# A hybrid decoder layer with 32 experts: expert weights stored as 16 KB runs and loaded in page pairs, 26 pages in place of 24

## The chip, the cores and the metric

The program runs on one core of a Trainium2 chip, as one launch, with all inputs in HBM. The metric is the device time of one launch in microseconds, the median of several; lower is better.

## The reference

One decoder layer over 256 tokens of 1024 numbers, all float32: projections of x, sparse attention (8 heads) and a gated linear recurrence (4 heads), an output projection, a layer norm, then a mixture of 32 experts of which each token uses 4, and a second layer norm. The change concerns the experts:

```python
logits = xf @ w_r + b_r
top_v, top_i = lax.top_k(logits, TOP_K)          # 4 of 32
top_w = jax.nn.softmax(top_v, axis=-1)
# for the rows xb of expert e:
h = xb @ w_gu[e] + b_gu[e]                       # w_gu[e]: 1024 x 2048
gate = jnp.minimum(h[:, :D_FF], SWIGLU_LIMIT)
up = jnp.clip(h[:, D_FF:], -SWIGLU_LIMIT, SWIGLU_LIMIT)
act = gate * jax.nn.sigmoid(SWIGLU_ALPHA * gate) * (up + 1.0)
y = act @ w_dn[e] + b_dn[e]                      # w_dn[e]: 1024 x 1024
```

An expert has 8.39 MB of w_gu and 4.19 MB of w_dn, 12.58 MB together; 32 experts are 402.7 MB.

## The kernel before

**Two stages.** First the attention and recurrence stage up to the router, about 205 us, whose order is found by a planner while the program is built: `Merge.run` (L205) picks among streams of work, on the planner's own clock, whichever can run next; a stream that asks for buffer space that is not there (`need`, L352) waits. Then the expert loop (L1740) in plain order: for each expert `gate_up` (L1577), `combine` of the expert before, for every second expert a `gather` of the rows of the next two, `scatter_lhs`, then `down` (L1611). The last expert (e31) is written apart (L1793 on), with its weights in smaller pieces.

**Pages.** Buffers come from 24 pages of 8 KB per partition (1 MB), each a tile of its own (class `Pages`, L224). A page can be cut into halves of 1024 and quarters of 512 words. One expert takes twelve pages: `g{e}_0` to `g{e}_7` for w_gu (a page holds 128 rows of 2048 numbers) and `d{e}_0` to `d{e}_3` for w_dn (256 rows of 1024, two to a partition). Twenty pages' worth goes round in the expert loop; two of the halves are used together as one page.

**Loads.** All weights come through one queue, SyncE's (SP). `want` (L367) puts loads in a list; `pump` (L370) issues from its head as long as a page is free, and is called whenever a buffer is freed (`Buf.free`, L344). `wg` and `wd` (L1750, L1758) free the page of the piece before when they ask for the next piece. An issue waits on the chip for the readers of its page, and also for the load that was issued eight loads earlier, since there are eight semaphores for SP's loads. In the first stage `GATE` holds loads back to times of the planner's clock.

**Layout.** `w_gu[e]` and `w_dn[e]` lie in HBM as the reference has them. A load of `g{e}_k` reads one run of 8 KB per partition, a load of `d{e}_k` two runs of 4 KB. For e31 the w_gu pieces have runs of 2 KB, the w_dn pieces runs of 2 KB and 1 KB, and most of these are issued as two or three loads (`fine`, L364).

Of the kernel before, what the change touches and what calls it, by code (L numbers as in the profile page):

```python
# [20 lines left out]
P = 128  # L21
# [8 lines left out]
RMS_EPS = 1e-6  # L30
GELU = float(2.0 * np.sqrt(2.0 / np.pi))
SET_LN_EXP = 'natural_log_exp_and_others'
NPAGES = 24
NR = 4
WARM = 30
GATE = {'wq0': 2.75, 'wq1': 5.75, 'wkg0': 8.75, 'wkg1': 11.5, 'wgh0': 14.5, 'wgh1': 17.5, 'wqa0': 20.25, 'wqa1': 23.25, 'wvs0': 26.25, 'wkv0': 29.0, 'wc00': 32.0, 'wc10': 35.0, 'wc01': 37.75, 'wc11': 40.75, 'wi0': 43.75, 'wi1': 46.5, 'wo2': 49.5, 'wo3': 61.75, 'wo0': 64.5, 'wo1': 69.75, 'bias': 86.0, 'xres': 87.5, 'ln1': 90.25, 'g0_0': 91.0, 'g0_1': 94.0, 'g0_2': 101.75, 'g0_3': 104.5, 'g0_4': 107.5, 'g0_5': 110.5, 'g0_6': 113.25, 'g0_7': 118.0, 'd0_0': 122.0, 'd0_1': 124.75, 'd0_2': 127.75, 'd0_3': 130.75, 'g1_0': 137.5, 'g1_1': 140.25, 'g1_2': 143.25, 'g1_3': 151.0, 'g1_4': 153.75, 'g1_5': 156.75, 'g1_6': 159.75, 'g1_7': 167.25}
# [10 lines left out]
WC_AT = 6  # L47
PARTS = ((4,), (5,), (6, 7))
ROUTER_AT = 'rec'
LAST = [(slice(k * 512, (k + 1) * 512), slice(0, 512), (4, 512)) for k in range(2)]  # L50
LAST += [(slice(None), slice(c, c + 256), (8, 256)) for c in (512, 768)]
# [176 lines left out]
class Pages:  # L228

    def __init__(self, pool, n, clock):
        self.pool, self.clock = pool, clock
        self.tiles, self.kind = [None] * n, [None] * n
        self.whole = list(range(n))
        self.part = {1024: [], 512: []}
        for pg in range(n):
            self.renew(pg, "G")

    def renew(self, pg, kind):  # L240
        if self.kind[pg] != kind:
            self.kind[pg] = kind
            self.tiles[pg] = self.pool.tile([P, 2048], F32, name=f"page{pg}", tag=f"page{pg}")
            self.clock.same[self.tiles[pg].tensor.name] = f"page{pg}"

    def halves(self):
        return 2 * len(self.whole) + len(self.part[1024])

    def fits(self, n, whole=False):
        return bool(self.whole or not whole and (len(self.part[1024]) >= max(1, n // 1024) or n == 512 and self.part[512]))  # L250

    def get(self, n, kind="G", last=False):
        if n == 2048:
            if not self.whole:
                return None
            pg = self.whole.pop(-1 if last else 0)
            self.renew(pg, kind)
            return (pg, 0, 2048)
        if not self.part[n]:
            up = self.get(2 * n, last=True)  # L260
            if up is None:
                return None
            pg, o, _ = up
            self.part[n] += [(pg, o), (pg, o + n)]
        pg, o = self.part[n].pop(0)
        return (pg, o, n)

    def put(self, key):
        pg, o, n = key
        if n == 2048:  # L270
            self.whole.append(pg)
            return
        mate = (pg, o ^ n)
        if mate in self.part[n]:
            self.part[n].remove(mate)
            self.put((pg, min(o, o ^ n), 2 * n))
        else:
            self.part[n].append((pg, o))

    def ap(self, key):  # L280
        pg, o, n = key
        return self.tiles[pg][:, o:o + n]


def shaped(ap, shape):
# [9 lines left out]
def layer(ctx: ExitStack, tc: tile.TileContext, a: dict, out: bass.AP, dbg=None, n_exp=NEXP, cap_limit=CAP):  # L295
# [64 lines left out]
        return Buf(words, key=key)  # L360


    queue, loaded = [], {}
    fine = {f"d{n_exp - 1}_0": ((0, 2), (2, 4)), f"d{n_exp - 1}_1": ((0, 2), (2, 4)), f"d{n_exp - 1}_3": ((0, 4), (4, 6), (6, 8)), "wf1": ((0, 2), (2, 4))}  # L364
    fine.update({f"g{n_exp - 1}_{k}": ((0, 1), (1, 2)) for k in range(KD)})

    def want(name, src, shape, kind="pre"):  # L367
        queue.append((name, src, shape, kind))

    def pump():  # L370
        while queue:
            name, src, shape, kind = queue[0]
            if name == "pk":
                queue.pop(0)
                sp.dma_start(cst, a["cst"])
                sp.dma_start(pk, a["pk"])
                sp.dma_start(ipk, a["ipk"])
                continue
            whole = kind == "pre" or kind == "small" and shape[2] == 2048
            if waiting or mg.now < GATE.get(name, 0.0) or not pages.fits(shape[2] if kind == "small" else 2048, whole):  # L380
                return
            if "att1" not in mg.fired and kind != "small" and pages.halves() - 2 < (RES if GATE else (4, 10)[kind == "exp"]):
                return
            queue.pop(0)
            if kind == "small":
                rows, cols, words_ = shape
                bf = Buf(words_)
                loaded[name] = ([bf], bf.ap[:rows, words_ - cols:])
                sp.dma_start(loaded[name][1], src)
                continue  # L390
            if kind == "pre":
                bf = Buf(2048)
                loaded[name] = ([bf], bf.v(*shape))
                sp.dma_start(loaded[name][1], src)
                continue
            n = shape[0] // 2
            bufs = [Buf(1024), Buf(1024)] if not pages.whole or HALVES and len(pages.part[1024]) > 1 else [Buf(2048)]
            rows, rest = src.shape[0], tuple(shape[1:])
            for u, v in fine.get(name, ((0, shape[0]),) if len(bufs) == 1 else ((0, n), (n, 2 * n))):
# [65 lines left out]


    cst = small("cst", [C_END])
    pkb, ipkb = buf(1024), buf(512)
    pk = pkb.ap[:, :B_END]
    ipk = ipkb.v(dt=I32)[:, :227]  # L470
    lvl, pos_i = shaped(ipk[:, :224].bitcast(U8), (7, 128)), ipk[:, 224:227]
# [46 lines left out]
    for e in range(n_exp):  # L518
        if e == max(n_exp - 2, 0):
            want("ln2", a["ln2"], (4, 512, 2048), "small")  # L520
        for k in range(KD):
            src, shape = a["w_gu"][e, k * 128:(k + 1) * 128, :].rearrange("p (j f) -> p j f", j=2), (2, FF)
            if e == n_exp - 1:
                src = a["w_gu"][e, k % 4 * 256:(k % 4 + 1) * 256, :].rearrange("(a p) (j f) -> p a j f", p=P, j=2)
                src, shape = src[:, :, :, k // 4 * 512:(k // 4 + 1) * 512], (2, 2, 512)
            want(f"g{e}_{k}", src, shape, "exp")
        for k in range(4):
            rows, cols, shape = (slice(k * 256, (k + 1) * 256), slice(None), (2, 1024)) if e < n_exp - 1 else LAST[k]
            want(f"d{e}_{k}", a["w_dn"][e, rows, cols].rearrange("(a p) d -> p a d", p=P), shape, "exp")

    queue.pop(0)
    wf0 = buf(2048)
# [264 lines left out]

    def queries_h():
        yield "q"
        qf = (yield from need(1024))  # L800
        hg["qf"] = qf
        for j in range(2):
            act.copy(qf.v(4, S)[:, 2 * j:2 * j + 2, :], res_bank["q"][j].rearrange("p (h t) -> p h t", h=2))
        drop(*res_bank["q"])
        mg.fire("qf")
# [646 lines left out]
    def gather_first(t):  # L1452
# [29 lines left out]
            dve.tensor_reduce(Wt[:, u, :], ohw.rearrange("p j e -> p e j"), AX.X, OP.add)  # L1482
        swzb = Buf(0, key=scratch["late"][0].key)
        swz.extend([swzb.v(4, 2, 128)[:, j] for j in range(2)])


    def start():
# [55 lines left out]
    alid = small("alid", [128])  # L1543
    pool.tensor_scalar(alid, ident, ALPHA, None, OP.mult)
    sbuf = [small(f"sw{j}", [2, CAP]) for j in range(2)]
    xgb = h1b["xg"].v(KD, 128)
    n_g, n_s = [1], [0]

# [140 lines left out]
    def fallback():  # L1689
# [5 lines left out]
        with tc.If(most > cap_limit):  # L1695
            with tc.For_i(0, n_exp, 1) as ei:
# [6 lines left out]
                def wg(k):  # L1703
                    w_ = wb[n[0] % 3].v()
                    n[0] += 1
                    sp.dma_start(w_, a["w_gu"][eds, k * 128:(k + 1) * 128, :].rearrange("a p f -> p (a f)"))
                    return [w_[:, :FF], w_[:, FF:]]

                def wd(fc):
                    if fc % 2 == 0:  # L1710
                        n[0] += 1
                    w_ = wb[n[0] % 3].v(2, 1024)
                    if fc % 2 == 0:
                        sp.dma_start(w_, a["w_dn"][eds, fc * 128:(fc + 2) * 128, :].rearrange("e (a p) d -> p (e a) d", p=P))
                    return w_[:, fc % 2, :]

                for rd in range(1, S // CAP):
# [130 lines left out]
def arrange(i):  # L1848
# [28 lines left out]
    a["w_gu"], a["w_dn"] = n["w_gate_up"][0], n["w_down"][0]  # L1877
# [17 lines left out]
```

## Time and profile before

| | us |
|---|---|
| median of 3 runs | 1165.85 |
| lowest, highest | 1162.73, 1166.91 |
| the profiled execution | 1166.2 |
| its span, first to last instruction | 1164.4 |
| TensorE (PE) busy | 1059.9 (91%) |
| VectorE, ScalarE, GpSimd busy | 294.7, 200.3, 75.8 |

The profile's page divides the span into 40 slices of 29.1 us: busy tenths of each engine, TensorE's granted clock, the mean busy share of the 16 DMA engines and the GB/s they moved. PE's busy time counts modelled ends of pipelined matmuls; what it waits for is better read from its timeline. The profiled execution stands 0.35 us above the median of the runs.

### The profile page before, as it was taken

To read this page: it belongs to the slowest core of one execution; us is meant where nothing else is said; L and a number is where in the kernel's file an instruction comes from. 1 tells how busy PE (TensorE), PEld (TensorE's weight loads), DVE (VectorE), ACT (ScalarE), POOL (GpSimd) and SP (SyncE) were. 2 spreads that over 40 slices of the span, in tenths; PEclk is the share of its full clock that TensorE was granted. 3 is DMA by queue.
4 is the path that set the end of the run, shared out by engine and by line. 5 is a ranking of instruction groups with operands and counts; after the bars stand their busy time and mean duration, and the time that the engine had idled before them with its cause. 6 is when DMAs were issued, how large, how long until landed. Compare 5 with 4: busy or idle time off the path is not lost. (4 is left out here: it accounts for less than half of the span.)

```text
span 1164.4 us, 13820 instructions
## 1 busy us (share of the span) xinstructions
PE 1059.9 (91%) x5714; PEld 494.0 (42%) x5714; DVE 294.7 (25%) x626; ACT 200.3 (17%) x418; POOL 75.8 (7%) x69
## 2 busy tenths in 40 slices
PE   8788889899999999999999999989898989898986
PEld 8677667334343343434343434333333333332343
DVE  5898886401111111111111111111111111111013
ACT  5565754101010100101010101000000010010101
POOL 5554120000000000000000000000000000000001
PEclk9999999899999999999999999999999999999998
DMA  9721737989999999999999999999999999999993
GB/s 360 320 77 69 290 122 300 386 323 379 415 416 416 416 418 416 417 416 418 416 416 416 417 417 414 418 415 417 417 415 417 415 416 417 416 417 417 413 384 111
DMA packets 85922, 430.04 MB, mean 369 GB/s; under 512 B 7512, under 2 KB 9816, under 8 KB 54496
## 3 DMA queue, kind: packets, MB, share of 16 engines
q1 hardware_dynamic: 85856, 429.13, 91.3%
q8 instruction: 46, 0.75, 0.3%
q14 instruction: 20, 0.16, 0.0%
HBM read 428.05 MB, written 1.05 MB: 369 GB/s over the span
## 5 line engine op out<-in xcount | busy, mean ns | idle before, releaser
L441 PE MATMUL bank<-page,page 128*64 128x512 f32 (+2 forms) x3412 | 753.6, 592 | 29.4 <-DMA page<-in_w_gu 16.7
L441 PEld LDWEIGHTS bank<-page,page 128*64 128x64 f32 (+1 forms) x3412 | 247.4, 142 | 499.1 <-issue 404.5
L1593 DVE TENSOR_SCALAR page<-bank 128x512 f32<-128x512 f32 (+1 forms) x33 | 22.3, 676 | 716.7 <-PE bank L441 716.7
L143 PE MATMUL bank<-page,page 128*128 128x256 f32 (+7 forms) x904 | 143.1, 340 | 10.5 <-DVE page L143 5.0
L143 PEld LDWEIGHTS bank<-page,page 128*128 128x128 f32 (+2 forms) x904 | 116.6, 185 | 27.7 <-DVE page L143 6.4
L1594 ACT ACTIVATE page<-page 128x512 f32<-128x512 f32 (+1 forms) x33 | 20.3, 616 | 462.1 <-DVE page L1593 462.1
L441 PE MATMUL bank<-G,page 128*128 128x128 f32 x480 | 57.6, 278 | 15.1 <-DVE G L1556 15.1
L441 PEld LDWEIGHTS bank<-G,page 128*128 128x128 f32 x480 | 54.7, 192 | 27.5 <-DVE G L1556 27.5
L1810 POOL TENSOR_TENSOR page<-page,page 128x320 f32<-128x320 f32 (+1 forms) x2 | 1.6, 790 | 991.4 <-DVE page L1817 991.4
L143 DVE TENSOR_TENSOR page<-page,page 128x512 fp32r<-128x512 f32 (+5 forms) x62 | 54.7, 922 | 24.7 <-ACT page L143 24.6
L143 POOL TENSOR_TENSOR page<-page,page 128x512 fp32r<-128x512 f32 (+4 forms) x35 | 53.1, 1531 | 90.7 <-ACT page L143 73.2
L1621 ACT COPY page<-bank 128x512 f32<-128x512 f32 x31 | 18.1, 585 | 231.5 <-PE bank L441 231.5
L143 ACT CAST page<-page 128x512 fp32r<-128x512 f32 (+3 forms) x71 | 43.7, 654 | 16.8 <-PE bank L143 10.0
L441 PE MATMUL bank<-cst,sw 128*64 128x128 f32 x256 | 22.0, 295 | 19.1 <-DVE sw L1571 19.1
L1607 ACT COPY page<-bank 128x512 f32<-128x512 f32 (+1 forms) x33 | 18.9, 572 | 77.9 <-PE bank L448 77.9
L1562 ACT COPY page<-bank 128x512 f32<-128x512 f32 x30 | 17.6, 585 | 84.0 <-PE bank L441 84.0
L1574 DVE COPY page<-bank 128x256 f32<-128x256 f32 x32 | 13.6, 425 | 68.4 <-PE bank L441 68.4
L441 PEld LDWEIGHTS bank<-cst,sw 128*64 128x64 f32 x256 | 13.7, 140 | 35.4 <-DVE sw L1571 31.3
L1595 DVE TENSOR_TENSOR page<-page 128x512 f32<-128x512 f32 (+1 forms) x33 | 22.3, 676 | 22.5 <-ACT page L1594 22.5
L143 PE MATMUL bank<-cst,page 128*128 128x128 f32 (+2 forms) x101 | 16.9, 293 | 9.7 <-DVE page L143 8.3
L441 PEld LDWEIGHTS <-i 96*64 96x64 bf16 x197 | 11.0, 109 | 28.2 <-issue 28.0
L1598 DVE SCALAR_TENSOR_TENSOR page<-page 128x512 f32<-128x512 f32 (+1 forms) x33 | 22.3, 676 | 1.1
(148 smaller groups left out, 440.2 us busy)
## 6 DMA issues: line engine op xcount, KB each, us to landing
page<-in_w_gu SPq DMA_DIRECT2D x226, 1024.0 KB, 17.6
page<-in_w_dn SPq DMA_DIRECT2D x112, 1024.0 KB, 17.7
page<-in_w_gu SPq DMA_DIRECT2D x60, 512.0 KB, 16.1
page<-in_w_dn SPq DMA_DIRECT2D x31, 512.0 KB, 15.2
page<-in_w_o SPq DMA_DIRECT2D x4, 1024.0 KB, 4.7
page<-in_w_q SPq DMA_DIRECT2D x2, 1024.0 KB, 9.8
page<-in_w_gh SPq DMA_DIRECT2D x2, 1024.0 KB, 13.3
page<-in_w_qa SPq DMA_DIRECT2D x2, 1024.0 KB, 14.3
```

Source lines behind the costliest of these rows:

```text
L143: r = f(*args, **kw)
L441: pe.matmul(o, l, r, start=start, stop=stop, skip_group_check=True)
L1562: act.copy(xg[:, 4 * q:4 * q + 4, :m * CAP], bk[q].rearrange("p (a b) -> p a b", a=4)[:, :, :m * CAP])
L1574: dve.tensor_copy(sz.rearrange("p a b -> p (a b)"), bk[0][:, :256])
L1593: dve.tensor_scalar(ga, hb[0][:, :n], 7.0, None, OP.min)
L1594: act.activation(sg_, ga, AF.Sigmoid, scale=1.702)
L1595: dve.tensor_tensor(sg_, sg_, ga, OP.mult)
L1598: dve.scalar_tensor_tensor(up, up, 1.0, sg_, OP.add, OP.mult)
L1607: act.copy(aT, bk[0][:, :n * 128].rearrange("p (c s) -> p c s", c=n))
L1621: act.copy(y, py)
L1810: pool.tensor_tensor(z, z, lnp[:, 0, c0:], OP.mult)
```

## The change

The four edits are these. The expert weights are laid out anew on the host: for e0 to e30, two neighbouring pieces (`g{e}_0` and `g{e}_1`, and so on) stand side by side, so that a partition's part of the two is one run of 16 KB; e31 has arrays of its own (`w_gl`, `w_dl`) in which each piece is a run of 8 KB per partition. The pages are tiles of 16 KB per partition, two pages to a tile, and there are 26 in place of 24, from descriptor space of dynamic DMAs that this program does not use (`SCRATCH`). In the expert loop `pump` loads two pieces with one DMA of 2 MB as soon as both pages of a tile are free; pieces of e0 and e1 may go alone. Last, some buffers of the first stage move: `qf` and the router's sums share a page that is set aside from the start, and `alid` and the two `sw` tiles lie in the second half of that page instead of in tiles of their own.

```diff
-NPAGES = 24
+NPAGES = 26
+LAX = 1
+SCRATCH = 1024
...
+    def renew(self, pair, kind):
+        if self.kind[pair] != kind:
+            self.kind[pair] = kind
+            self.tiles[pair] = self.pool.tile([P, 4096], F32, name=f"page{pair}", tag=f"page{pair}")
...
+    def usable(self, kind="G"):
+
+        return [pg for pg in self.whole if self.kind[pg // 2] == kind or pg ^ 1 in self.whole]
+
+    def pairs(self):
+        return [pg for pg in self.whole if pg ^ 1 in self.whole and self.whole.index(pg ^ 1) < self.whole.index(pg)]
...
+    def get(self, n, kind="G", last=False, near=None, apart=False):
+
+        if n == 4096:
+            two = self.pairs()
+            if not two:
+                return None
+            pg = two[0] & ~1
+            self.whole.remove(pg)
+            self.whole.remove(pg + 1)
+            self.renew(pg // 2, kind)
+            return (pg, 0, n)
...
-            bufs = [Buf(1024), Buf(1024)] if not pages.whole or HALVES and len(pages.part[1024]) > 1 else [Buf(2048)]
+            bufs = None
+            if kind == "exp" and name[0] in "gd" and mates.get(name):
+                other = mates[name][0]
+                if int(name[-1]) % 2 == 0 and mg.now >= 1e6:
+                    key = pages.get(4096)
+                    if key is None and int(name[1:-2]) > LAX:
+                        queue.insert(0, (name, src, shape, kind))
+                        return
+                    if key is not None:
+                        queue.pop(0)
+                        two = [Buf(0, key=(key[0] + i, 0, 2048)) for i in range(2)]
+                        sp.dma_start(pages.ap(key), mates[name][1])
+                        for nm, b_ in zip((name, other), two):
+                            loaded[nm] = ([b_], [shaped(b_.ap[:, o:], (n,) + tuple(shape[1:])) for o in (0, 1024)])
+                        continue
+                near = loaded[other][0][0].key[0] ^ 1 if other in loaded else None
+                key = pages.get(2048, near=near, apart=near is None)
+                bufs = key and [Buf(0, key=key)]
+            if not bufs:
+                bufs = [Buf(2048)] if pages.usable() else [Buf(1024), Buf(1024)]
...
-    pkb, ipkb = buf(1024), buf(512)
+    pkb = buf(1024)
+    qf_late = pages.get(2048, near=pkb.key[0] ^ 1)
+    ipkb = buf(512)
...
+                src, shape = a["w_gl"][k].rearrange("p (a j f) -> p a j f", a=2, j=2), (2, 2, 512)
+            else:
+                src, shape = a["w_gu"][e, k // 2, :, k % 2 * 2048:k % 2 * 2048 + 2048].rearrange("p (j f) -> p j f", j=2), (2, FF)
+                mates[f"g{e}_{k}"] = (f"g{e}_{k ^ 1}", a["w_gu"][e, k // 2])
...
-        qf = (yield from need(1024))
+        qf = Buf(0, key=(qf_late[0], 0, 1024))
...
-        scratch["late"][0] = yield from need(1024)
+        scratch["late"][0] = Buf(0, key=(qf_late[0], 1024, 1024))
...
+    a["w_gu"] = gu.reshape(NEXP, 4, 2, P, 2 * FF).transpose(0, 1, 3, 2, 4).reshape(NEXP, 4, P, 4 * FF)
+    a["w_dn"] = dn.reshape(NEXP, 2, 4, P, D).transpose(0, 1, 3, 2, 4).reshape(NEXP, 2, P, 4 * D)
...
+    nc = bacc.Bacc("TRN2", target_bir_lowering=False, num_devices=1, dynamic_dma_scratch_size=SCRATCH)
```

**Place 1, SP's queue in the middle of the loop.** One expert's loads before; `page15_1795` is page 15, `128x2048` the elements written.

```order
L404 DMA page9_75<-in_w_gu 128x2048
L404 DMA page15_1795<-in_w_gu 128x2048
L404 DMA page2_1821<-in_w_gu 128x2048
L404 DMA page20_1857<-in_w_gu 128x2048
L404 DMA page14_1859<-in_w_gu 128x2048
L404 DMA page18_84<-in_w_gu 128x2048
L404 DMA page6_72<-in_w_gu 128x2048
L404 DMA page19_85<-in_w_gu 128x2048
L404 DMA page0_1301<-in_w_gu 128x2048
L404 DMA page3_1331<-in_w_dn 128x2x1024
L404 DMA page4_1363<-in_w_dn 128x2x1024
L404 DMA page5_1395<-in_w_dn 128x2x1024
```

The same place in the changed kernel, where a page name is a pair of pages.

```order
L436 DMA page0_1321<-in_w_gu 128x4096
L436 DMA page2_1386<-in_w_gu 128x4096
L436 DMA page9_75<-in_w_gu 128x4096
L436 DMA page3_69<-in_w_gu 128x4096
L436 DMA page5_71<-in_w_dn 128x4096
L436 DMA page10_76<-in_w_dn 128x4096
```

Twelve loads of 1 MB have become six of 2 MB, and the tiles that go round are eleven pairs, 22 MB, in place of 20 MB.

**Place 2, SP's queue where the first stage ends.** Rows of L143 (before) are issued by the first stage, rows of L404 by the expert loop.

```order
L143 DMA page2_1821<-in_w_gu 128x2048
L143 DMA page20_1857<-in_w_gu 128x2048
L143 DMA page14_1859<-in_w_gu 128x2048
L404 DMA page18_84<-in_w_dn 128x2x1024
L404 DMA page6_72<-in_w_dn 128x2x1024
L404 DMA page19_85<-in_w_dn 128x2x1024
L404 DMA page0_1301<-in_w_dn 128x2x1024
L404 DMA page3_1331<-in_w_gu 128x2048
```

After, with L144 the line of the first stage, and L451 and L436 lines of the loop:

```order
L144 DMA page7_1812<-in_w_gu 128x2048 x2
L144 DMA page11_77<-in_w_dn 128x2048
L144 DMA page4_70<-in_w_dn 128x2048
L451 DMA page6_72<-in_w_dn 128x2048 x2
L436 DMA page8_74<-in_w_gu 128x4096
L436 DMA page0_1321<-in_w_gu 128x4096
```

Two pieces more, `d1_0` and `d1_1`, are asked for before the loop; from the weights of e2 on all loads up to e30 are pairs.

**Place 3, ScalarE (ACT) in the first stage.** The rows with `sm` are a head's softmax exponentials, the CASTs of 128x512 make the split operands of projections, and the eight COPYs of 64x128 move transposed blocks for the recurrence. Before:

```order
L143 ACTIVATE page_74,sm_949<-bank_90,mx_948 128x128 x2
L143 ACTIVATE page_74,sm_949<-bank_97,mx_948 128x128 x2
L143 CAST page_102<-page_76 128x512 x2
L143 COPY page_88<-bank_96 64x128 x8
L143 CAST page_103<-page_78 128x512
L143 ACTIVATE page_74,sm_989<-bank_91,mx_988 128x128 x2
```

After:

```order
L144 ACTIVATE page_69,sm_910<-bank_81,mx_909 128x128 x2
L144 ACTIVATE page_69,sm_910<-bank_82,mx_909 128x128 x2
L144 CAST page_89<-page_69 128x512 x3
L144 COPY page_76<-bank_86 128x2x128
L144 ACTIVATE page_77,sm_964<-bank_80,mx_963 128x128 x2
L144 ACTIVATE page_77,sm_964<-bank_85,mx_963 128x128 x2
L144 CAST page_89<-page_69 128x512
L144 COPY page_75<-bank_79 64x128 x8
```

The eight copies now stand behind the second head's exponentials instead of between the first and the second; the same work stands in another order there, and so on PE and VectorE beside it.

## Rows read from the trace of the kernel before

**Rows 1.** The page: PE's busy time, DMA share and rate by slice.
```profile
PE 1059.9 (91%) x5714; PEld 494.0 (42%) x5714; DVE 294.7 (25%) x626; ACT 200.3 (17%) x418; POOL 75.8 (7%) x69
DMA  9721737989999999999999999999999999999993
GB/s 360 320 77 69 290 122 300 386 323 379 415 416 416 416 418 416 417 416 418 416 416 416 417 417 414 418 415 417 417 415 417 415 416 417 416 417 417 413 384 111
```
**Rows 2.** PE's timeline of the loop: start, length in us, tiles; brackets: idle before.
```profile
319.74 3.84 PE L441 MATMUL bank<-G,page 128*128 128x128 f32 x32 [1.01 <-DVE G L1556]
...
375.73 3.84 PE L441 MATMUL bank<-G,page 128*128 128x128 f32 x32 [1.00 <-DVE G L1556]
...
431.76 3.84 PE L441 MATMUL bank<-G,page 128*128 128x128 f32 x32 [1.00 <-DVE G L1556]
...
605.61 7.09 PE L441 MATMUL bank<-page,page 128*64 128x512 f32 x32 [0.38 <-ACT page L1607]
...
631.73 8.78 PE L441 MATMUL bank<-page,page 128*64 128x512 f32 x32 [0.34 <-ACT page L1607]
...
760.33 1.94 PE L441 MATMUL bank<-page,page 128*64 128x512 f32 x8 [0.43 <-DMA page<-in_w_gu]
...
1075.78 3.84 PE L441 MATMUL bank<-G,page 128*128 128x128 f32 x32 [1.01 <-DVE G L1556]
```
**Rows 3.** PE's waits: what for, us in total, times, longest.
```profile
PE bank L143 <- DVE page L143: 19.3, 10, 3.5
...
PE bank L441 <- DMA page<-in_w_gu: 16.7, 28, 1.4
```
**Rows 4.** Windows: busy us of PE, PEld, DVE, ACT, POOL; clock; DMA share; GB/s.
```profile
0.00:205.00 205.00, 176.15 (x1209) 149.27 (x1209) 157.44 (x328) 115.99 (x275) 72.31 (x65) 0.96 0.57 221
...
265.00:275.00 10.00, 9.66 (x58) 4.21 (x59) 0.42 (x1) 1.88 (x4) 0.00 (x0) 1.00 0.86 307
275.00:300.00 25.00, 23.63 (x112) 8.07 (x110) 3.55 (x7) 1.67 (x3) 0.00 (x0) 0.93 1.01 414
300.00:760.00 460.00, 437.89 (x2258) 171.37 (x2254) 60.01 (x128) 38.74 (x65) 0.00 (x0) 1.00 1.02 416
760.00:1075.00 315.00, 283.96 (x1420) 105.11 (x1420) 39.65 (x84) 24.47 (x41) 0.00 (x0) 0.99 1.02 416
...
1112.00:1130.00 18.00, 15.11 (x92) 7.29 (x93) 0.37 (x1) 1.17 (x2) 0.00 (x0) 0.91 1.05 386
```
**Rows 5.** The page's DMA sections: packets by size, packets by queue, issues by size.
```profile
DMA packets 85922, 430.04 MB, mean 369 GB/s; under 512 B 7512, under 2 KB 9816, under 8 KB 54496
...
q8 instruction: 46, 0.75, 0.3%
...
page<-in_w_gu SPq DMA_DIRECT2D x226, 1024.0 KB, 17.6
```
**Rows 6.** SP's issues of g4, then PE's gate_up of e4, from the timeline.
```profile
282.17 19.13 SPq L404 DMA_DIRECT2D page<-in_w_gu  x10
...
332.78 15.82 PE L441 MATMUL bank<-page,page 128*64 128x512 f32 x72
```
**Rows 7.** Loads by tensor, issue to landing: w_gu first, then w_o.
```profile
DMA to landing us min/median/max: 4.7/17.5/21.4
...
DMA to landing us min/median/max: 4.6/4.7/6.4
```
**Rows 8.** The end: SP's last weight loads; PE's last products of down.
```profile
1123.48 14.64 SPq L404 DMA_DIRECT2D page<-in_w_dn  x8
...
1150.76 2.95 PE L441 MATMUL bank<-page,page 128*64 128x256 f32 x19
```

More of the change, by code (lines that the diff above doesn't have):

```diff
@@ L49 @@
 ROUTER_AT = 'rec'
-LAST = [(slice(k * 512, (k + 1) * 512), slice(0, 512), (4, 512)) for k in range(2)]
-LAST += [(slice(None), slice(c, c + 256), (8, 256)) for c in (512, 768)]
+LAST = [(4, 512), (4, 512), (8, 256), (8, 256)]
 LAST_ORDER = (("p", 0), ("a", 0), ("p", 1), ("p", 2), ("a", 1), ("a", 2))
@@ L233, in __init__ @@
         self.pool, self.clock = pool, clock
-        self.tiles, self.kind = [None] * n, [None] * n
+        self.tiles, self.kind = [None] * (n // 2), [None] * (n // 2)
         self.whole = list(range(n))
         self.part = {1024: [], 512: []}
[L237 to L244, printed above, removed]
+        for pair in range(n // 2):
+            self.renew(pair, "G")
@@ new lines, in renew @@
+    def renew(self, pair, kind):
+        if self.kind[pair] != kind:
+            self.kind[pair] = kind
+            self.tiles[pair] = self.pool.tile([P, 4096], F32, name=f"page{pair}", tag=f"page{pair}")
+            self.clock.same[self.tiles[pair].tensor.name] = f"page{pair}"
+    def usable(self, kind="G"):
+        return [pg for pg in self.whole if self.kind[pg // 2] == kind or pg ^ 1 in self.whole]
+    def pairs(self):
+        return [pg for pg in self.whole if pg ^ 1 in self.whole and self.whole.index(pg ^ 1) < self.whole.index(pg)]
@@ L246, in halves @@
     def halves(self):
-        return 2 * len(self.whole) + len(self.part[1024])
+        return 2 * len(self.usable()) + len(self.part[1024])
     def fits(self, n, whole=False):
-        return bool(self.whole or not whole and (len(self.part[1024]) >= max(1, n // 1024) or n == 512 and self.part[512]))
-    def get(self, n, kind="G", last=False):
+        return bool(self.usable() or not whole and (len(self.part[1024]) >= max(1, n // 1024) or n == 512 and self.part[512]))
+    def get(self, n, kind="G", last=False, near=None, apart=False):
[8 more added lines that the diff above has]
+            return (pg, 0, n)
@@ L253, in get @@
         if n == 2048:
-            if not self.whole:
-                return None
-            pg = self.whole.pop(-1 if last else 0)
-            self.renew(pg, kind)
-            return (pg, 0, 2048)
+            ok = self.usable(kind)
+            if not ok:
+                return None
+            single = [pg for pg in ok if pg ^ 1 not in self.whole]
+            double = [pg for pg in ok if pg ^ 1 in self.whole]
+            first = (double or single) if apart else (single or double)
+            pg = near if near in ok else first[-1 if last else 0]
@@ L259, in get @@
+            self.whole.remove(pg)
+            self.renew(pg // 2, kind)
+            return (pg, 0, n)
         if not self.part[n]:
@@ L269, in put @@
         pg, o, n = key
+        if n == 4096:
+            self.whole += [pg, pg + 1]
+            return
         if n == 2048:
@@ L281, in ap @@
         pg, o, n = key
-        return self.tiles[pg][:, o:o + n]
+        o += pg % 2 * 2048
+        return self.tiles[pg // 2][:, o:o + n]
 def shaped(ap, shape):
@@ L360, in need @@
         return Buf(words, key=key)
-    queue, loaded = [], {}
+    queue, loaded, mates = [], {}, {}
     fine = {f"d{n_exp - 1}_0": ((0, 2), (2, 4)), f"d{n_exp - 1}_1": ((0, 2), (2, 4)), f"d{n_exp - 1}_3": ((0, 4), (4, 6), (6, 8)), "wf1": ((0, 2), (2, 4))}
@@ L396, in pump @@
             n = shape[0] // 2
-            bufs = [Buf(1024), Buf(1024)] if not pages.whole or HALVES and len(pages.part[1024]) > 1 else [Buf(2048)]
+            bufs = None
[5 more added lines that the diff above has]
+                        queue.insert(0, (name, src, shape, kind))
+                        return
+                    if key is not None:
[10 more added lines that the diff above has]
+                bufs = [Buf(2048)] if pages.usable() else [Buf(1024), Buf(1024)]
             rows, rest = src.shape[0], tuple(shape[1:])
@@ L520, in layer @@
             want("ln2", a["ln2"], (4, 512, 2048), "small")
+        last = e == n_exp - 1
         for k in range(KD):
[L522 to L525, printed above, removed]
+            if last:
+                src, shape = a["w_gl"][k].rearrange("p (a j f) -> p a j f", a=2, j=2), (2, 2, 512)
+            else:
+                src, shape = a["w_gu"][e, k // 2, :, k % 2 * 2048:k % 2 * 2048 + 2048].rearrange("p (j f) -> p j f", j=2), (2, FF)
+                mates[f"g{e}_{k}"] = (f"g{e}_{k ^ 1}", a["w_gu"][e, k // 2])
             want(f"g{e}_{k}", src, shape, "exp")
         for k in range(4):
-            rows, cols, shape = (slice(k * 256, (k + 1) * 256), slice(None), (2, 1024)) if e < n_exp - 1 else LAST[k]
-            want(f"d{e}_{k}", a["w_dn"][e, rows, cols].rearrange("(a p) d -> p a d", p=P), shape, "exp")
+            if last:
+                shape = LAST[k]
+                src = a["w_dl"][k].rearrange("p (a d) -> p a d", a=shape[0])
+            else:
+                src, shape = a["w_dn"][e, k // 2, :, k % 2 * 2048:k % 2 * 2048 + 2048].rearrange("p (a d) -> p a d", a=2), (2, 1024)
+                mates[f"d{e}_{k}"] = (f"d{e}_{k ^ 1}", a["w_dn"][e, k // 2])
+            want(f"d{e}_{k}", src, shape, "exp")
     queue.pop(0)
@@ L1484, in gather_first @@
         swz.extend([swzb.v(4, 2, 128)[:, j] for j in range(2)])
+        h1b["small"] = [swzb.v(8, 128)[:, j] for j in range(4, 8)]
     def start():
@@ L1542, in layer @@
     acc = take(4)
-    alid = small("alid", [128])
+    alid, *sbuf = h1b["small"][:3]
+    sbuf = [shaped(z, (2, CAP)) for z in sbuf]
     pool.tensor_scalar(alid, ident, ALPHA, None, OP.mult)
-    sbuf = [small(f"sw{j}", [2, CAP]) for j in range(2)]
     xgb = h1b["xg"].v(KD, 128)
@@ L1705, in wg @@
                     n[0] += 1
-                    sp.dma_start(w_, a["w_gu"][eds, k * 128:(k + 1) * 128, :].rearrange("a p f -> p (a f)"))
+                    sp.dma_start(w_, a["w_gu"][eds, k // 2, :, k % 2 * 2048:k % 2 * 2048 + 2048].rearrange("a p f -> p (a f)"))
                     return [w_[:, :FF], w_[:, FF:]]
@@ L1713, in wd @@
                     if fc % 2 == 0:
-                        sp.dma_start(w_, a["w_dn"][eds, fc * 128:(fc + 2) * 128, :].rearrange("e (a p) d -> p (e a) d", p=P))
+                        sp.dma_start(w_, a["w_dn"][eds, fc // 4, :, fc % 4 * 1024:fc % 4 * 1024 + 2048].rearrange("e p (a d) -> p (e a) d", a=2))
                     return w_[:, fc % 2, :]
@@ L1876, in arrange @@
         a[k] = np.concatenate([n[k + "_g"][0], n[k + "_b"][0]]).reshape(4, 512)
-    a["w_gu"], a["w_dn"] = n["w_gate_up"][0], n["w_down"][0]
+    gu, dn = n["w_gate_up"][0], n["w_down"][0]
+    a["w_gu"] = gu.reshape(NEXP, 4, 2, P, 2 * FF).transpose(0, 1, 3, 2, 4).reshape(NEXP, 4, P, 4 * FF)
+    a["w_dn"] = dn.reshape(NEXP, 2, 4, P, D).transpose(0, 1, 3, 2, 4).reshape(NEXP, 2, P, 4 * D)
+    a["w_gl"] = gu[-1].reshape(4, 2, P, 2, 2, 512).transpose(4, 0, 2, 1, 3, 5).reshape(8, P, 2048)
+    dl = dn[-1].reshape(8, P, D).transpose(1, 0, 2)
+    a["w_dl"] = np.stack([z.reshape(P, 2048) for z in (dl[:, :4, :512], dl[:, 4:, :512], dl[:, :, 512:768], dl[:, :, 768:])])
     quarters = lambda v: v.reshape(NEXP, 4, -1).transpose(1, 0, 2).reshape(P, -1)
@@ L1887 @@
     arrays = {f"in_{k}": v for k, v in arrange(inputs).items()}
-    nc = bacc.Bacc("TRN2", target_bir_lowering=False, num_devices=1)
+    nc = bacc.Bacc("TRN2", target_bir_lowering=False, num_devices=1, dynamic_dma_scratch_size=SCRATCH)
     a = {k[3:]: nc.dram_tensor(k, v.shape, mybir.dt.from_np(v.dtype), kind="ExternalInput").ap() for k, v in arrays.items()}
```

## The prediction

> **What bounds the kernel now.** I read the page first [rows 1]: TensorE (PE) is busy 91% of the span, which looks like a bound, but the DMA engines are full as well, at about 416 GB/s from the eleventh slice to the last but two. Which of the two sets the pace is read from PE's timeline [rows 2]. The gather of rows (PE reading G) comes once in two experts, so the distance of two gathers is PE's period. From 375.73 to 431.76 it is 56.03 us, with no wait for a load. Two experts bring 25.17 MB, and at 416 GB/s [rows 4] that takes 60.5 us. So PE eats faster than the DMA feeds: 28.01 us an expert against 30.25. What hides that at first is the stock in the pages. g4 is issued from 282.17 on, lands some 17.5 us later by the median of w_gu [rows 7], that is from about 300, and is used from 332.78 [rows 6]: about 30 us ahead. Each expert takes 2.24 us of this, and the clock dips give a little back, so the stock should last some 14 to 15 experts. The first wait of PE for w_gu in the loop is at 760.33 [rows 2], in e19: 15 experts later. From then on the DMA sets the pace; the waits are short (28 of them, 16.7 us in all, the longest 1.4 [rows 3]), since each is only the difference of two rates, and each also breaks the overlap of neighbouring matmuls.
>
> What these waits cost in all is read from the gathers: from 319.74 to 1075.78 are 13 periods, 756.0 us; 13 × 56.03 are 728.4; the clock dips take part of the rest (32 matmuls of down in 8.78 us in place of 7.09 [rows 2], twice in this stretch, 3.4 us). There remain **24.2 us** that loads cost PE. After 1075.78, PE has no wait for a load: the last weight loads are issued from 1123.48 for 14.64 us, and the last products stand at 1150.76 [rows 8]. Before 205 us the DMA is busy 57% [rows 4], and PE waits for VectorE and ScalarE.
>
> **Longer runs.** The page counts 85,922 packets, 54,496 of them under 8 KB [rows 5]. Of the 31,426 others, 226 whole w_gu loads of 128 runs of 8 KB make 28,928, and the 1 MB loads of the first stage the rest: one packet for one run. What a packet costs beside its bytes follows from two stretches in which the 16 engines are full. From 1112 to 1130 us runs of 2 KB are moved (w_gu of e31) at 386 GB/s [rows 4]: 2048 B × 16 / 386 GB/s = 84.9 ns a packet on its engine. In the steady stretch one expert is 64 packets of 8 KB and 64 of 4 KB on each engine in 30.25 us, so one of each takes 472.6 ns. With time = a + b × bytes, the two give a = 9.2 ns and b = 0.0370 ns per byte (433 GB/s over 16 engines). A packet of 16 KB would then take 615 ns, and an expert 48 × 615 = 29.51 us (426 GB/s): **0.73 us less for each expert**. Ends: if a run of 16 KB were cut into packets of 8 KB, only w_dn would gain: 32 packets less on each engine, 0.29 us. With no cost for a packet at all, 12.58 MB at 433 GB/s take 29.06 us, 1.19 less. I take 0.73: the instruction queue moved 0.75 MB in 46 packets [rows 5], 16 KB each, so the engines do take packets of that size.
>
> The Trainium skill, DMA: Bandwidth & Descriptors, "Why small descriptors are slow (HBM only)", gives a fixed cost of about 3 bus cycles for a packet, at the 850 MHz of the same page 3.5 ns by my estimate; this trace shows 9.2 ns. By the page's figure the 80 packets that an expert loses on each engine are worth 0.28 us, and the sum below would end at 1158.9.
>
> **How much of it reaches the end.** From about 275 us the DMA never stops [rows 4]. While PE still waits for loads at the end of the loop, e29's weights arrive earlier by what the DMA saved on all loads from there on: e4 to e29, 26 experts × 0.73 = **19.0 us**. The limit is the 24.2 us that loads cost at all; 19.0 is below it, so a few short waits of PE should be left, from about e26 on. e31's loads get faster too (runs of 4 KB in place of 2 and 1 KB; by the fit 161 ns for 4 KB against 2 × 84.9), 1 to 2 us, but PE does not wait for them now, so I cost that at nothing; what hides it is the distance between landing and use at the end [rows 8], which moves with the DMA.
>
> **Two pages more, and pairs.** The loop goes round 22 MB in place of 20. At the last point where the DMA waits for pages (265 to 275 us, 307 GB/s [rows 4]) it is 2 MB further, worth 4.9 us at 426 GB/s. Pairs take it back: a 2 MB load is issued when the second page is free, and then runs 4.9 us where the second page alone took 2.5: 2.4 us. And its first half can be used only when the second has landed: another 2.4. I take nothing, with ends of −2.5 and +4.9 us. SP issues half as many loads, and a wait of SP for a pair holds up only later weight loads, as everything in that queue is. SP's wait for the load issued eight loads earlier now allows 16 MB in flight instead of 8, more than it needs. `alid` and `sw` in other tiles change no operation in the loop: nothing.
>
> **The first stage.** The planner's order has changed, on PE, VectorE and ScalarE (place 3), because buffer space comes free at other times. The amount of work is the same, and `qf` and the router's sums no longer ask for space. PE is busy 176.15 of the 205 us [rows 4]; its waits for VectorE are 19.3 us in 10, the longest 3.5 [rows 3]. No row tells which waits the new order makes. I take nothing, and for the ends one of the longest waits more or less, ±3.5 us. What is lost here shifts the whole loop; a part would come back where loads still make PE wait.
>
> **Sum.** The profiled execution took 1166.2 us; 1166.2 − 19.0 = **1147**. It stands 0.35 above the median of the runs, which is less than I can tell.
>
> **Rivals.**
> *All waits go* (PE bound): the saving is 24.2 or more, because two more pages count (up to 4.9) or a packet costs more than 9.2 ns. Then PE runs from gather to gather in 56.03 us to the end, and the time is 1166.2 − 24.2 = 1142. For it: 19.0 + 4.9 is almost there. Against: pairs give that back. And at 29.06 us, with packets that cost nothing, the DMA would still be slower than PE.
> *Runs cut at 8 KB, or a packet cost smaller than the fit's*: 26 × 0.29 = 7.6, time 1158.6. Against it the 16 KB packets of the instruction queue [rows 5].
> *The change does nothing to the rate*: 416 GB/s is what HBM gives and not the packets. Then only e31's pieces and the pages are left, 0 to 5 us: 1161 to 1166. Against it: the rate does depend on run length, 386 against 416 [rows 4].
> *Slower, by the rows' distance*: neighbouring partitions lie 16 KB apart, and if the 16 engines then meet in the same part of HBM, the rate falls. Each 1% under 416 costs 0.30 us an expert, 7.9 us over 26; at 413 GB/s the time is 0.5% worse, at 400 GB/s it is 1.2 × 26 = 31 us worse, 1198. Against it: w_o is read as runs of 8 KB that lie 32 KB apart, and lands in 4.7 us, as fast as the fastest w_gu load [rows 7]. The Trainium skill, DMA page, "Latency and other measured facts", lists a loss from row pitches that are large powers of two; its smallest pitch, 512 KiB, loses little, and no run here has such a pitch.
> *Slower, by the first stage*: the new order doubles PE's idle time there, 28.9 us [rows 4], more than the loads give: about 1171. It decides from some 25 us on; against it, that would be eight times the longest single wait.
>
> **How the numbers follow.** Forecast (1144 to 1150): 0.45. All waits gone, 1142 with the first stage's ±3.5: 0.22. Cut or cheap packets, near 1158: 0.13. Rate unchanged, 1161 to 1166: 0.09. Slower by HBM 0.04, by the first stage 0.04. Better than 1139 by a luckier first stage: 0.03. The range 1139 to 1159 holds the first three. A measurement of this kernel can tell about 0.5% (5.8 us) from no change: faster 0.82, same 0.10, slower 0.08.
>
> **What would show it.** In the profile after: expert packets of 16 KB, the packet count near 41,000; 425 to 428 GB/s in the middle slices; 30.25 us for 12.58 MB turned into 29.5; gathers 56.0 us apart well beyond 760 us, and PE's waits for w_gu few and late, a few us in all. The gather of e30's rows, at 1075.78 now, should come near 1057. If the middle slices still show 416 the packet argument is wrong; if the rate is right and the time is not, look at where the first gate_up starts (205 us now). If PE waits though the rate rose, the pairs cost more stock than two pages give.

## The result and the profile after

The changed kernel takes 1145.32 us (median of 4 runs, 1143.80 to 1146.04), against 1164.49 for the kernel before on the same chip: a ratio of 0.983, 95% interval 0.981 to 0.986. That is 19.2 us less; the forecast was 19 less, at 1147. The profiled execution took 1145.62 us, its span is 1143.8.

The page after, in the sections of [rows 1, 5]: busy time, DMA share and rate by slice, packets, and the loads by size.

```profile
PE 1052.6 (92%) x5714; PEld 498.7 (44%) x5714; DVE 290.2 (25%) x625; ACT 199.9 (17%) x418; POOL 74.4 (7%) x70
...
DMA  8832744979999999999999999999999999999991
GB/s 333 322 148 88 279 168 177 429 297 386 429 427 427 428 427 427 427 429 428 426 429 427 428 425 430 427 427 425 429 428 427 426 428 429 429 427 427 423 388 55
DMA packets 37518, 430.00 MB, mean 376 GB/s; under 512 B 4168, under 2 KB 4424, under 8 KB 9552
...
page<-in_w_gu SPq DMA_DIRECT2D x116, 2048.0 KB, 32.8
page<-in_w_dn SPq DMA_DIRECT2D x58, 2048.0 KB, 30.2
```

The bytes are the same, 430.0 MB, in 37,518 packets where 85,922 were. Of 16 KB there were 46 before, those of the instruction queue; the trace now holds 22,318, the 46 and 128 for each of the 174 loads of 2 MB. The middle slices show 427 GB/s where 416 stood. PE's busy share has hardly moved, and would not have told any of this.

PE's timeline of the loop after, beside [rows 2]: gathers, and the first wait for a load.

```profile
318.24 3.84 PE L488 MATMUL bank<-G,page 128*128 128x128 f32 x32 [1.01 <-DVE G L1613]
...
878.68 3.84 PE L488 MATMUL bank<-G,page 128*128 128x128 f32 x32 [1.01 <-DVE G L1613]
...
926.07 3.65 PE L488 MATMUL bank<-page,page 128*64 128x512 f32 x16 [1.13 <-DMA page<-in_w_gu]
...
1055.39 3.84 PE L488 MATMUL bank<-G,page 128*128 128x128 f32 x32 [1.01 <-DVE G L1613]
```

From 318.24 to 878.68 are ten periods of 56.04 us, PE's own pace without one wait for a load. The first wait comes at 926.07 and no longer at 760.33. The gather of e30's rows has moved from 1075.78 to 1055.39, 20.4 us earlier; what follows it is 88.4 us long and was 88.6. So the gain lies in the loop alone. Thirteen periods are 737.15 us, 8.6 more than 13 × 56.04: that is what loads still cost PE, where it was 24.2. The waits after, beside [rows 3]:

```profile
PE bank L144 <- DVE page L144: 13.6, 12, 2.5
...
PE bank L488 <- DMA page<-in_w_gu: 7.1, 6, 1.2
```

Six waits in place of 28, and each stands before 16 matmuls and not 8: a pair lands as one. The same stretches as in [rows 4]:

```profile
0.00:205.00 205.00, 179.16 (x1204) 151.92 (x1205) 152.45 (x326) 115.41 (x274) 70.91 (x66) 0.93 0.58 221
...
230.00:275.00 45.00, 43.50 (x210) 17.82 (x212) 4.44 (x11) 3.56 (x6) 0.00 (x0) 0.93 0.79 317
...
300.00:760.00 460.00, 437.90 (x2266) 171.50 (x2264) 60.05 (x128) 38.74 (x65) 0.00 (x0) 1.00 1.01 428
...
1090.00:1110.00 20.00, 16.46 (x106) 8.92 (x108) 1.36 (x4) 1.17 (x2) 0.00 (x0) 0.91 1.03 406
```

The first stage has the same length: the first gate_up starts at 205.71 us and started at 205.15. The last row is e31, whose w_gu now comes in runs of 4 KB, at 406 GB/s; with runs of 2 KB it was 386.

### The profile page after: what moved, and what is told of

Read it like the earlier page. It is cut to its first block, busy times and chain, and to the rows that moved or that the text cites. A ratio compares the mean times of both kernels' runs of the same rounds, so it can differ in the third digit from the quotient of the medians.

```text
span 1143.8 us, 13393 instructions
## 1 busy us (share of the span) xinstructions
PE 1052.6 (92%) x5714; PEld 498.7 (44%) x5714; DVE 290.2 (25%) x625; ACT 199.9 (17%) x418; POOL 74.4 (7%) x70
## 2 busy tenths in 40 slices
DMA packets 37518, 430.00 MB, mean 376 GB/s; under 512 B 4168, under 2 KB 4424, under 8 KB 9552
## 5 line engine op out<-in xcount | busy, mean ns | idle before, releaser
L488 PE MATMUL bank<-page,page 128*64 128x512 f32 (+2 forms) x3160 | 682.6, 586 | 18.5 <-ACT page L1664 11.4
L488 PEld LDWEIGHTS bank<-page,page 128*64 128x64 f32 (+1 forms) x3160 | 226.7, 138 | 436.6 <-issue 388.9
L144 PE MATMUL bank<-page,page 128*128 128x256 f32 (+6 forms) x836 | 131.2, 335 | 9.3 <-ACT page L144 4.9
L144 PEld LDWEIGHTS bank<-page,page 128*128 128x128 f32 (+2 forms) x836 | 108.0, 189 | 24.5 <-ACT page L144 6.9
L488 PE MATMUL bank<-page 64*128 64x512 f32 (+2 forms) x260 | 65.8, 608 | 0.9 <-ACT page L1701 0.7
L144 POOL TENSOR_TENSOR page<-page,page 128x512 fp32r<-128x512 f32 (+4 forms) x37 | 54.9, 1500 | 76.1 <-ACT page L144 64.1
L144 DVE TENSOR_TENSOR page<-page,page 128x512 fp32r<-128x512 f32 (+6 forms) x58 | 47.9, 861 | 29.1 <-ACT page L144 28.9
L144 ACT CAST page<-page 128x512 fp32r<-128x512 f32 (+3 forms) x71 | 43.6, 654 | 23.2 <-PE bank L144 13.8
L488 PEld LDWEIGHTS bank<-page 64*128 64x128 f32 (+1 forms) x260 | 23.3, 186 | 42.5 <-issue 40.8
L144 PE MATMUL bank<-page 128*128 128x128 f32 (+4 forms) x182 | 33.1, 325 | 7.3 <-DVE page L144 4.9
L488 PE MATMUL bank<-cst,page 128*64 128x128 f32 x256 | 22.0, 295 | 19.0 <-DVE page L1628 19.0
L144 PEld LDWEIGHTS bank<-page 128*128 128x128 f32 x182 | 26.2, 197 | 11.0 <-DVE page L144 3.6
L1631 DVE COPY page<-bank 128x256 f32<-128x256 f32 x32 | 13.6, 425 | 68.4 <-PE bank L488 68.4
L488 PEld LDWEIGHTS bank<-cst,page 128*64 128x64 f32 x256 | 13.7, 140 | 35.3 <-DVE page L1628 31.2
```

Of the source, the lines that this page charges most:

```text
L144: r = f(*args, **kw)
L488: pe.matmul(o, l, r, start=start, stop=stop, skip_group_check=True)
L1631: dve.tensor_copy(sz.rearrange("p a b -> p (a b)"), bk[0][:, :256])
```

## The experiments

Theory: the cost of a packet sets the DMA's rate, and the DMA sets where the loop ends. Rivals: that two more pages, or fewer and larger loads, made the gain; that runs above 8 KB do nothing; that PE's late waits have another cause.

**The old runs in the new pages.** Everything of the change stays, 26 pages, 2 MB loads, order; only the layout in HBM of e0 to e30 is that of before.

```diff
-                        sp.dma_start(pages.ap(key), mates[name][1])
+                        sp.dma_start(shaped(pages.ap(key), mates[name][1].shape[1:]), mates[name][1])
...
+                mates[f"g{e}_{k}"] = (f"g{e}_{k ^ 1}", a["w_gu"][e, k // 2 * 256:k // 2 * 256 + 256, :].rearrange("(j p) f -> p j f", j=2))
...
+                mates[f"d{e}_{k}"] = (f"d{e}_{k ^ 1}", a["w_dn"][e, k // 2 * 512:k // 2 * 512 + 512, :].rearrange("(a p) d -> p a d", p=P))
...
+    a["w_gu"], a["w_dn"] = gu, dn
```

> The changed kernel with its 26 pages, its 2 MB loads and its order, but the weights of e0 to e30 lie in HBM as before, so that a 2 MB load reads runs of 8 KB (w_gu) and 4 KB (w_dn). Theory (packets set the DMA's rate, and the DMA sets the end): the rate falls back to 416 GB/s, an expert takes 30.25 us instead of 29.4, and over 26 experts that is 21 us: about 1166, with PE waiting for w_gu again from about 760 us on. Rival (two more pages, or fewer and larger loads, made the gain): it stays at 1145 to 1150.

Measured: 1162.86 us, ratio to the kernel before 0.998 (0.997 to 0.999). The gain is gone, and with it the rate. A window of the steady stretch, and PE's first wait:

```profile
300.00:760.00 460.00, 436.08 (x2248) 170.35 (x2244) 60.00 (x128) 38.74 (x65) 0.00 (x0) 1.00 1.02 417
```
```profile
755.26 1.94 PE L488 MATMUL bank<-page,page 128*64 128x512 f32 x8 [0.76 <-DMA page<-in_w_gu]
...
1074.43 1.83 PE L488 MATMUL bank<-G,page 128*128 128x128 f32 x14 [1.01 <-DVE G L1613]
```

417 GB/s, waits from 755 us on, e30's gather at 1074.43. Pages, pairs, larger loads, e31's layout and the new order of the first stage together are worth the remaining 0.2%, 1 to 3 us; the run's length is worth the difference of the two ratios, 0.0152 or 17.7 us. The larger loads add nothing to the rate that shows: 2 MB loads with the old runs move 417 GB/s, 1 MB loads did 416. The one between them has another source. Of the 248 w_gu pieces of e0 to e30 the kernel before loads 226 whole and 22 into two halves, each with runs of 4 KB, so that an expert is 133 packets on each engine (packet records of 300 to 760 us) and not the 128 of the prediction and of this run. Five packets of 9 ns are 0.05 us an expert and 1.2 us over 26, most of what is left here.

**24 pages.** `NPAGES = 24`, nothing else.

> The changed kernel with 24 pages in place of 26: ten pairs go round. Theory: the rate stays at 427 GB/s; the stock is 2 MB smaller, worth 4.9 us of DMA, while PE still waits at the end: about 1150, with the new order of the first stage adding up to 3.5 us either way. Rival (the pages made the gain): 1158 or more, near the kernel before.

Measured: 1153.12 us, ratio 0.990 (0.989 to 0.992): 8 us behind the changed kernel, where 4.9 was expected. Windows:

```profile
230.00:250.00 20.00, 19.85 (x80) 7.32 (x82) 0.53 (x2) 1.17 (x2) 0.00 (x0) 0.85 0.12 37
250.00:275.00 25.00, 23.65 (x132) 10.48 (x130) 3.95 (x9) 2.38 (x4) 0.00 (x0) 1.00 1.01 430
300.00:760.00 460.00, 437.93 (x2258) 171.32 (x2256) 60.01 (x128) 38.74 (x65) 0.00 (x0) 1.00 1.01 427
```

The rate is the same, but from 230 to 250 us, while PE works between the gate_up of e0 and of e1 and frees little, the DMA almost stands still: 37 GB/s where the changed kernel has 259. SP's longest wait for PE there is 26.1 us, and 17.5 in the changed kernel. Over the whole stretch from 205 to 300 us the DMA moves 335 GB/s in place of 377: 4.0 MB less, 9.3 us of DMA. e30's gather comes at 1064.73, just these 9.3 us later; what follows it is 86.7 us long and not 88.4 (a clock dip less, see the end), which leaves 8. The order of the first stage costs nothing here (first gather at 262.34 against 262.24).

It is not the missing pages alone that stop the DMA. The kernel before has 24 pages too, but loads single ones, and there the same 20 us show 281 GB/s:

```profile
230.00:250.00 20.00, 19.85 (x80) 6.87 (x78) 0.42 (x1) 1.17 (x2) 0.00 (x0) 0.85 0.74 281
```

The standstill comes of few pages and pairs together.

**Pairs as two loads.** Each pair is loaded by two loads of 1 MB, runs of 8 KB, into the same pages.

```diff
-                        sp.dma_start(pages.ap(key), mates[name][1])
+                        for i in range(2):
+                            sp.dma_start(pages.ap(key)[:, i * 2048:i * 2048 + 2048], mates[name][1][:, i * 2048:i * 2048 + 2048])
```

> The changed kernel, but each pair is loaded by two loads of 1 MB with runs of 8 KB, one behind the other into the same two pages; nothing else is changed. By the fit of 9.2 ns a packet, 96 packets an expert take 29.96 us instead of 29.43: 13.8 us over 26 experts, less 2.4 for the first half that lands earlier: about 1156. If the packet cost between 8 and 16 KB is smaller than the fit (half of it), about 1149. If the length of a run above 8 KB does nothing: 1143.

Measured: 1154.72 us, ratio 0.991 (0.990 to 0.993), next to the 1156 of the fit. The steady window:

```profile
300.00:760.00 460.00, 437.93 (x2258) 171.32 (x2256) 60.01 (x128) 38.79 (x65) 0.00 (x0) 1.00 1.01 421
```

So three kernels with different runs give the packet's cost apart from the fit. An expert takes 12.58 MB / 417 = 30.18 us with 128 packets on each engine, / 421 = 29.89 with 96, / 427.5 (the middle of 427 and 428) = 29.43 with 48. From 128 to 96 that is 0.29 us / 32 = 9.0 ns a packet, from 96 to 48 0.46 / 48 = 9.5 ns; the fit had 9.2. A step of 1 GB/s in the rates is 0.07 us, so each of the two is known to about 2 ns.

The kept traces hold a record of each packet, and these need no fit. From 300 to 760 us a packet of 4 KB takes 164 ns on the mean (kernel before, and old runs), one of 8 KB 314 to 315 (these two, split pairs, no pairs), one of 16 KB 616 (changed kernel). The records overlap a little, so that two of 8 KB less one of 16 KB, 12 ns, is more than the packet costs in time. The 8 KB runs lie side by side in HBM in the kernel before and 16 KB apart in the split pairs, and take the same; so it is their length that counts and not where they lie. A packet and a run are one here: whether the time goes with the one or with the other, no run tells.

The 3.5 ns worked out from the Trainium skill, DMA: Bandwidth & Descriptors, "Why small descriptors are slow (HBM only)", do not hold here; on the same page "Rules for kernel authors" asks for loads of 1 MiB or more, which nearly all loads up to e30 have in both kernels, and puts no price on the length of a run.

**Less to load.** From e2 to e30 only the first half of each w_dn pair is loaded; the products of the other half are computed with what the page held before.

```diff
-                        sp.dma_start(pages.ap(key), mates[name][1])
+                        w_ = 2048 if name[0] == "d" else 4096
+                        sp.dma_start(pages.ap(key)[:, :w_], mates[name][1][:, :w_])
```

> The changed kernel, but from e2 to e30 only the first half of each w_dn pair is loaded; the other half of the page keeps what lay there, so this part of the products is left wrong. The DMA then has 10.5 MB an expert, 24.6 us at 427 GB/s, less than PE's 28.0. Theory: PE's waits for w_gu (8.6 us with what they add between gathers) go, and nothing else: 1137, with gathers 56.0 us apart to the end, and any clock dips of 1.7 us each on top. Rival (PE's late waits are not the DMA's rate): no change, 1145.

Measured: 1137.39 us. The waits for w_gu are gone from the list, and the gathers keep their distance to the end:

```profile
992.38 1.83 PE L489 MATMUL bank<-G,page 128*128 128x128 f32 x14 [1.00 <-DVE G L1614]
...
1048.42 1.83 PE L489 MATMUL bank<-G,page 128*128 128x128 f32 x14 [1.01 <-DVE G L1614]
```

56.04 us. From the first gather of the loop (260.51) to e30's are 14 periods, 787.9 us: 14 × 56.04 and two clock dips of 1.7. So about 1137 is where PE alone would end, and some 8 us is what the loads still cost the changed kernel. That it hits the 1137 so closely is in part luck: between the two profiled executions the waits' 8.6 us went and the two dips added 3.4, while the loop began 1.7 us earlier and what follows e30's gather was 1.5 us shorter.

**More singles at the start.** `LAX = 3`: e2 and e3 may take single pages too.

> The changed kernel with LAX = 3 in place of 1: the weights of e2 and e3 too are loaded as single pages while no pair is free. Theory (the stock that the first experts leave counts as long as PE waits for loads at the end): from 230 to 275 us the DMA moves more than 317 GB/s, since a load starts when one page is free and one page more is used, 2 to 5 us of DMA; two experts with runs of 8 KB cost 2 x 0.4 us. PE's late waits shrink by the difference: about 1142. Rival (the pairs cost no stock): 1145 to 1146.

Measured: 1145.42 us, against 1144.66 for the changed kernel run beside it: no gain, a miss. The windows tell where the stock went:

```profile
230.00:250.00 20.00, 19.85 (x80) 6.60 (x80) 0.00 (x0) 1.07 (x2) 0.00 (x0) 0.92 0.91 335
250.00:275.00 25.00, 23.65 (x134) 10.59 (x132) 3.95 (x9) 2.97 (x5) 0.00 (x0) 1.00 0.94 376
275.00:300.00 25.00, 23.63 (x120) 8.32 (x118) 3.55 (x7) 1.80 (x3) 0.00 (x0) 1.00 0.93 370
```

The DMA does move more from 230 to 275 us (335 and 376 GB/s against 259 and 364, 1.8 MB), but when the loop goes back to pairs it has to wait for both pages of a pair, and 370 GB/s stand from 275 to 300 where the changed kernel has 430: 1.5 MB are given back. By 350 us nothing is left: from 205 on both kernels have moved 394 GB/s. PE's timeline of this run, e30's gather, and two places behind it where the clock was low:

```profile
1054.20 2.05 PE L488 MATMUL bank<-G,page 128*128 128x128 f32 x16 [1.00 <-DVE G L1613]
...
1066.95 4.73 PE L488 MATMUL bank<-page,cst 4*128 4x512 f32 x8
...
1093.24 8.78 PE L488 MATMUL bank<-page,page 128*64 128x512 f32 x32 [0.34 <-ACT page L1664]
```

The gather came 1.2 us earlier than in the first profile of the changed kernel (1.6 than in the second), no more than the loop began earlier in this execution (first gate_up at 203.48 and not 205.71); but what follows it is 90.9 us long and not 88.4. The eight products in the second row take 3.69 us in the changed kernel; the dip in the third stands there in e31 instead (below). That accounts for 1 us of the 2.5; the rest was not followed.

**No pairs.** `LAX = 99`: every load is one page, 24 MB go round.

> The changed kernel with LAX = 99: no pairs at all, every load is a single page with a run of 8 KB, as soon as a page is free, and 24 MB go round in place of 22. Rate as with split pairs, 421 GB/s. Theory: 1154.7 with split pairs, less 2.4 to 4.9 us for the page or two more and 2.4 for waiting on no pair: about 1149. Rival (with pages enough, the length of runs above 8 KB is worth nothing): 1145.

Measured: 1151.46 us, ratio 0.989 (0.987 to 0.992), at 421 GB/s: 3.3 us better than pairs in two loads (2.4 by the two ratios, whose intervals overlap), where 4.8 to 7.3 were expected, and 6.8 behind the changed kernel. The early windows agree with the 3.3: from 205 to 300 us 392 GB/s against 376, 1.5 MB or 3.6 us. From 230 to 250 us single loads never starve:

```profile
230.00:250.00 20.00, 19.85 (x82) 7.11 (x80) 0.42 (x1) 1.17 (x2) 0.00 (x0) 0.86 0.89 341
```

Freer paging is worth less than longer runs.

**One part alone.** The kernel before with w_dn in runs of 8 KB, 24 pages, single loads.

```diff
+            src = a["w_dp"][e, k].rearrange("p (a d) -> p a d", a=2) if e < n_exp - 1 else a["w_dn"][e, rows, cols].rearrange("(a p) d -> p a d", p=P)
...
+    a["w_dp"] = n["w_down"][0].reshape(NEXP, 4, 2, P, D).transpose(0, 1, 3, 2, 4).reshape(NEXP, 4, P, 2 * D)
```

> The kernel before, with one edit: w_dn of e0 to e30 is laid out so that a piece is one run of 8 KB per partition instead of two of 4 KB. 24 pages, single loads, the order of before, e31 as before. Theory: the rate is that of 8 KB runs, 421 GB/s, 29.9 us an expert instead of 30.25, 26 x 0.36 = 9 us: about 1155. Rival (only the whole change gives something): 1164.

Measured: 1158.69 us, ratio 0.995 (0.993 to 0.996), at 420 GB/s in the steady stretch. The sign and the rate are right, but 5.9 us came of 9; the runs spread from 1153 to 1160. The profiled execution, 1154.89, is one of the fastest, and a part of its lead is not the layout's: its first gather of the loop comes at 258.50 and not 262.05, with the order of the first stage unchanged. From the first to the last gather it has 806.1 us, 7.6 less than before (813.7). Why the median keeps less than that is open.

**The changed kernel once more**, beside the last three:

> The changed kernel again, beside the three others: 1145 to 1146, gathers as in its first profile; the clock dips may fall elsewhere, and while the DMA sets the end of the loop they should not change the time.

Measured: 1144.66 us, ratio 0.983 (0.981 to 0.985). In this profile a clock dip falls into the loop (granted clock 0.58 from 686 to 690 us, 0.99 and 1.00 in the ten after):

```profile
686.43 8.78 PE L488 MATMUL bank<-page,page 128*64 128x512 f32 x32 [0.34 <-ACT page L1664]
...
880.42 1.83 PE L488 MATMUL bank<-G,page 128*128 128x128 f32 x14 [1.01 <-DVE G L1613]
...
1055.78 1.49 PE L488 MATMUL bank<-G,page 128*128 128x128 f32 x11 [1.01 <-DVE G L1613]
```

At 880.42 PE is 1.74 us later than in the first profile (878.68), as much as a dip costs; at e30's gather only 0.39 us are left. While PE waits for loads at the end, a dip ahead of that is paid from the stock.

None of these beats the changed kernel with the whole computation done.

## Why the prediction was right

**What bounds.** Two rates, 28.0 us an expert for PE and 30.25 for the DMA, with a stock between them: right. With the DMA's load cut below PE's pace the waits went, and the gathers stood at PE's own distance but for two clock dips (1137.39); with the old runs all but 1 to 3 us came back.

**The packet's cost.** The fit from two stretches of the trace before gave 9.2 ns and 426 GB/s for runs of 16 KB, 420 for 8 KB; measured were 427 to 428, and 421, and the packets' own records have 616 ns for 16 KB where it had 615. That one run of 16 KB is one packet, argued from the instruction queue, holds by the 22,318 packets of 16 KB; the count of all, 37,518, is under the 41,000 named. The rivals "cut at 8 KB", "no effect on the rate" and "slower by the rows' distance" fall with the same rows, and "all waits go" with the six waits that are left.

**How much reaches the end.** 26 × 0.73 = 19.0 us; e30's gather moved by 20.4. The term is right, and a little small: it counted 128 packets for an expert in the kernel before where the halves make it 133. With 133 the same two stretches give 9.4 ns, and 85 packets less are 0.80 us an expert, 20.8 over 26. The measured worth of the runs alone, 17.7 us, lies on the other side; in the profiled executions e30's gather moved by 19.0 us for it (1074.43 with the old runs), and the changed kernel lost 1.6 of them behind that gather (88.4 us against 86.8), as much as one clock dip. The short waits that should be left were 5.2 us (24.2 − 19.0) from e26 on; they are 8.6 us, and from e25 on, one expert earlier than said. What the gathers gained besides is clock dips: between the first and the last gather the trace before has three of 1.7 us, this one none. I had kept the dips out of the sum as PE's own time, which is not so while the DMA paces the end: there they are paid from the stock, as the repeated run shows. The whole is therefore read from the DMA's saving, and not from the waits and dips apart.

**Pages and pairs.** Taken at nothing, and the sum of both was nearly that: 1.4 us by the run with the old runs, and 1.2 of these belong to the halves. The prediction got there by pricing the two apart, pages by their bytes (4.9 us) and pairs by the time of a load (4.9), and this step does not hold: a page is worth more where loads come in pairs. What the DMA moved from 205 to 300 us tells it: 335 GB/s with 24 pages in pairs and 377 with 26, 367 with 24 single pages (the kernel before) and 392 with 26 (no pairs). So two pages bring 4.0 MB with pairs, the 8 to 9 us of that run, where SP waits 26.1 us for a pair and the DMA stops. With single loads they bring at most 2.4 MB, of which up to 0.5 come of the faster rate: about the 2 MB that was reckoned. Pairs take back 1.4 MB with 26 pages, 3.3 us, where 2.4 were said for the later issue, and 3.0 MB with 24. The other 2.4, for a first half that lands with the second, no run measures by itself. That the sum came out near nothing is in part luck.

**The first stage.** Taken at nothing, ±3.5: the first gate_up starts 0.6 us later, the first gather of the loop 0.2 us. Single executions of one order spread by more: the first gate_up stands at 203.48 and 205.71 in two kernels with the new order, at 202.78 and 205.15 in two with the old. So the runs bear out that the new order costs little, and not a finer number. PE's waits for VectorE are 5.7 us shorter there (13.6 against 19.3), which the time does not show: PE is busy 3.0 us longer, at a granted clock of 0.93 in place of 0.96, and its waits for ScalarE are 2.3 us longer (7.2 against 4.9).

## What to carry to other kernels

Where DMA engines are full and runs are 2 to 16 KB long, read the cost of a packet from two stretches with different runs and multiply it by the packets that a new layout saves; here some 9 ns a packet were 1.5% of the kernel, and the size of a load counted for nothing. How much of a faster feed is seen is read from the consumer's own period and its stock: it is the feed's saving, as long as the consumer still waits at the end, and no more than its waits. A coarser unit of buffer space takes back part of what it gives, and more of it the less space there is; price unit and space together, at the place where the consumer frees least.

## What the runs showed of the hardware

The rate went on rising with the length of the runs, from 386 GB/s at 2 KB over 406 at 4 KB and 421 at 8 KB to 427 at 16 KB. And PE's clock dips cost 1.7 us each and fall at other places in other runs of one kernel. Behind e30's gather they show in the time, since no load is waited for there. The gate_up of e31's first half, in the changed kernel and then in the run with less w_dn:

```profile
1102.42 8.79 PE L488 MATMUL bank<-page,page 128*64 128x256 f32 x64
```
```profile
1095.59 7.10 PE L489 MATMUL bank<-page,page 128*64 128x256 f32 x64
```

1.7 us apart for the same products; the granted clock in the first is 0.66 from 1102 to 1107 us and 1.00 from 1107 to 1112, where 1.00 is 2.4 GHz. What sets where the dips fall was not tried.
